# Background products of a Hymba block at every fourth step of the big matmuls, two pairs of heads side by side

## The chip, the cores and the metric

One core of one Trainium2 chip runs one launch of the kernel. The time is device microseconds for the launch. TensorE (PE in the profile) does matmuls, VectorE (DVE) and ScalarE (ACT) work on elements, GpSimd (POOL) and SyncE (SP) mostly issue transfers. Each engine works through its instructions in a fixed order; an instruction that waits holds up all that stand behind it on its engine.

## The reference

One layer of a decoder block on 512 tokens of width 2048, all in float32:

```python
h = rmsnorm(x) * (1 + scale1(c)) + shift1(c)
p = h @ w_in                                  # 2048 columns for the conv group, 3520 for RWKV
# A: val * sigmoid(gate), causal depthwise conv of 31 taps, group norm, silu       (16 heads of 64)
# B: token shift, then per head of 64:  S = S * w + (S a) b^T + v k^T ;  y = S r   (16 heads, 512 tokens)
#    group norm of y, + bonus (sum of r * k * r_k) * v, times the gate g
x = x + gate1(c) * (concat[A, B] @ w_out)
h = rmsnorm(x) * (1 + scale2(c)) + shift2(c)
x = x + gate2(c) * ((silu(h @ w1) * (h @ w3)) @ w2)      # d_ff = 5632
return rmsnorm(x)
# scale, shift and gate: six blocks of 2048 columns of c @ w_ada + b_ada
```

## The kernel before

**Big matmuls.** Every large product is done as three fp32r matmuls (high times high, high times low, low times high; `mm3`, line 74 does each). Weights arrive as 128x1024 blocks; `split` rounds a block on ACT (`wh`, line 92) and takes the rest on DVE (`wl`, line 93). A *step* is the work of one weight block on one accumulator, three matmuls with 512 columns. The program is a list of units of 16 steps: `in_units` (w_in, 37 units, 1776 big matmuls in the order `ORDER`), `out_units` (w_out, 16 units, 256 steps), `fast_units` (w1 and w3, a Strassen-like form) and `ff2_units` (w2).

**Background work.** All else of the mixer runs in the shadow of the steps. It is cut into generators that yield between pieces, and a `Lane` advances one generator: it waits as many steps as its table of waits says, then lets the next piece issue its instructions. Four lanes run at once. `scan` does `rwkv_scan` for a pair of heads, in halves of eight chunks of 64 tokens: products named `fp` and `yy` on TensorE, then `FV` (lines 780, 781) and the state `S` (line 792) on DVE. `pre` does `rwkv_pre` for the next pair: scaled keys, the masked products `gg`, `bk` and `npp`, transposes (line 639), and `inverse` of a triangular matrix. In the inverse, a 16x16 part is solved on DVE, goes through DRAM, is widened on POOL (`a`, line 719), and is then grown by a chain of products in the buffer `gg`. `cnv` does the 31 taps on DVE (line 843) and the norm of two heads of the conv group. `ada` makes rows or columns of the modulation, 512 columns per job: 16 multiply-adds of 128x512 on DVE (line 882), each on a block `wa` loaded from `w_ada`, and at the end a product with ones. The tables are `SCAN`, `PRE`, `CONV`, `ADA` and, in w_out, `ADA_ROWS`. Small products go to buffers `bk` (two), `gg` (one), `fp` and `yy`.

**Order.** `run()` sends the units through `stream`, and after every step it runs each lane once. A scheduler then places the instructions of each engine, and so the final order on an engine is not that of the code alone; it is shown below where it matters.

**Around w_out.** In unit 3 of w_out's first column block, `open_ff` finishes the first three lanes at once. Then four jobs remain: three rows of gate1 (column blocks 1 to 3), which `add_row` needs when a column block of w_out is done, and one job (`LATE = 1`) that makes the last quarter of `s2`, the columns of 1 + scale2. `open_h2`, ahead of the first ff1 unit, finishes what is left, folds `norm2_g` into `s2`, transposes x for tokens 0 to 255 (`make_a`, line 1108, scaled and shifted by `s2` and `sh2` into `raw`, line 1115) and makes the first ff1 operands. `scale` multiplies x by the row's rstd (line 1074). At the end of ff1, `last_hid` rounds the last hidden block into `hh` and `hl` for ff2, at a place named in the table `todo`.

Of the kernel before, what the change touches and what calls it, by code (L numbers as in the profile page):

```python
# [20 lines left out]
NT = T // P  # L21
CW = 1024
NB = CW // P
# [12 lines left out]
class Block:  # L36
# [912 lines left out]
    def run(self):  # L949
# [27 lines left out]
        pres = []  # L977
# [3 lines left out]
        for n, ps in zip("rkv", first):  # L981
# [4 lines left out]
        pres.append((0, dict(self.rkv)))  # L986
        self.gate = {}
        ada = lambda part, cc, out, fn: fn(part, cc, out)
        self.scan, self.pre, self.cnv = Lane(self.scans, self.rwkv_scan, SCAN), Lane(pres, self.rwkv_pre, PRE, PRE0), \
            Lane(self.convs, self.conv, CONV)  # L990
        lanes = self.lanes = [self.scan, self.pre, self.cnv, Lane(adas, ada, ADA)]


        def in_units():
# [28 lines left out]
        def open_ff():  # L1023
            own = lanes[:3]
            while any(l.busy for l in own):
                for l in own:
                    next(l)
            del lanes[:3]
            self.mix_back(KB)
            rps.close()  # L1030
            lops.close()
            self.xp = tops.enter_context(tc.tile_pool(name="xp", bufs=1))
            self.ff = ffs.enter_context(tc.tile_pool(name="ff", bufs=1))

            self.x1 = []
            load_x(0)
            self.rows = self.ff.tile([P, D], F32, name="rows", bufs=1)
            self.ss = self.ff.tile([P, NT, 8], F32, name="ss", bufs=1)[:, :, 0:4]
            rows = [(2, cc, lambda: self.rows, self.ada_rows) for cc in range(1, 4)]
            lanes[0].queue.extend(rows + late)  # L1040
            lanes[0].waits = lanes[0].first = ADA_ROWS
            self.fast_ws = fasts.enter_context(tc.tile_pool(name="wsp2", bufs=1, side="right"))

        def open_rows():
# [25 lines left out]
        def scale(c, t, engine):  # L1070
            o, rs = self.x1[c][:, t], self.rs[:, t:t + 1]
            if engine is nc.scalar:
                return engine.activation(out=o, in_=o, func=AF.Identity, scale=rs)
            return engine.tensor_scalar(out=o, in0=o, scalar1=rs, scalar2=None, op0=ALU.mult)
# [77 lines left out]
        def fast_units():  # L1152
            v, s = nc.vector, nc.scalar
            for c in range(NF // 4):
# [61 lines left out]
                for part in range(2):  # L1216
                    for u in range(4):
                        def stepped(j, part=part, u=u, c=c, turn=turn, end0=end0, end1=end1):
                            if c == 0 and part == 0 and u < 3 and j == 0:
                                for t in range(NT):  # L1220
                                    scale(u + 1, t, nc.scalar if u else nc.vector)
                            if c == 0 and part == 0 and u == 0 and j in (4, 5):
                                make_a(j - 4, (1,))
                            if c == 0 and part == 0 and u < 3 and j in (2, 7):
                                make_a(2 * u + 2 + j // 7)
                            if c == 0 and part == 0 and u == 3 and j in (7, 9):
                                make_b(j // 9)
                            if c == 0 and part == 1 and u < 3 and j in (1, 7):
                                make_b(2 * u + 2 + j // 7)
                            if c and part == 0 and u in (1, 2) and j in (1, 6):  # L1230
                                turn(2 * (u - 1) + j // 6)
                            if u == 3:
                                (end0, end1)[part](j)
# [20 lines left out]
        def get4(k):  # L1254
            f["four"] = k, self.ff.tile([P, 4, T], F32, name="hr", bufs=1)
            nc.gpsimd.dma_start(out=f["four"][1], in_=self.raw[k:k + 4].rearrange("k p t -> p k t"))
# [33 lines left out]

        def ff2_units():

            todo = {(0, 0, 0): [open_ff2], (0, 0, 4): [last_hid, load_x1, load_x1],
                    (0, 0, 8): [lambda: get4(12), load_x1, load_x1], (0, 1, 0): [lambda: split4(12), lambda: get4(16)],
                    (0, 1, 8): [lambda: split4(KB), lambda: get4(20)], (0, 3, 4): [lambda: split4(0), lambda: get4(24)],
                    (0, 3, 8): [lambda: split4(4), lambda: get4(28)], (1, 0, 0): [lambda: split4(8), lambda: get4(32)],
                    (1, 3, 8): [lambda: split4(12), lambda: get4(36)], (1, 3, 12): [lambda: split4(KB)]}
# [39 lines left out]
            yield from fast_units()  # L1337
            yield from ff2_units()

        for _ in self.stream(units()):  # L1340
            for l in lanes:
                l.run()

# [6 lines left out]

SCAN = (2, 2, 2, 3, 1, 1, 2, 3, 1, 1, 3, 2, 2, 2, 2, 2, 2, 1, 3, 2, 2)
PRE = (2, 2, 2, 2, 2, 2, 2, 2, 2, 2, 1, 2, 2, 2, 2, 3, 2, 8, 4, 2, 2, 2, 2, 1, 2, 2, 2, 1, 2)
CONV = (2, 2, 2, 2, 1, 2, 1, 2, 3, 3, 2, 2, 2, 2, 2, 2, 2, 3)
ADA = (4, 4, 4, 4, 4, 4, 4, 4, 4, 4, 4, 4, 4, 4, 4, 4, 4, 4, 6, 3, 3, 3)
ADA_ROWS = (2, 1, 2, 2, 2, 2, 2, 2, 3, 2, 3, 2, 2, 2, 2, 3, 2, 2, 4, 4, 2, 2)
PRE0 = PRE[:17] + (20,) + PRE[18:]  # L1360
LATE = 1

WS2 = 6
# [2 lines left out]
class Lane:  # L1366


    def __init__(self, queue, fn, waits, first=None):
        self.queue, self.fn, self.waits, self.first = queue, fn, waits, first or waits  # L1370
        self.job, self.n, self.wait, self.done = None, 0, 0, 0

    @property
    def busy(self):
        return bool(self.job or self.queue)

    def run(self):
        if self.wait:
            self.wait -= 1
        else:  # L1380
            next(self)

    def finish(self, n):

# [131 lines left out]
```

## Time and profile before

| what | value |
|---|---|
| median of 3 runs | 2484.78 us (2482.81 to 2487.75) |
| profiled execution | 2477.18 us, its span 2475.5 us |
| TensorE busy | 2373.9 us, 96% of the span |
| VectorE busy | 1784.8 us, 72% |
| ScalarE busy | 1048.3 us, 42% |
| head, up to the first w_in unit behind it | 0 to 158.6 us |
| w_in | 158.6 to 876.5 us |
| w_out | 876.5 to 1093.7 us |
| entry to ff1 | 1093.7 to 1104.0 us |
| ff1 | 1104.0 to 1983.2 us |
| ff2 | 1983.2 to 2475.5 us |

The span runs from the first instruction to the last one; the profiled execution lasts 1.7 us longer. The stages are read off TensorE's timeline by the names of its matmuls. A busy TensorE is not TensorE at its best: matmuls overlap one another, and their ends are modelled, so that the cost of a small product is read from the starts of the big matmuls on either side of it.

### The profile page before, as it was taken

Reading aid. Unit: us, or ns where it says so; the run is one execution under the profiler, and the core shown is the slowest. Engines: PE = TensorE matmul, PEld = TensorE weight load, DVE = VectorE, ACT = ScalarE, POOL = GpSimd, SP = SyncE. Lnnn points to the kernel's source line nnn. Section 1 sums busy time; section 2 is a strip of 40 time slices with the busy share of each in tenths; the row PEclk is TensorE's granted clock in tenths of the full one; section 3 lists DMA queues with packets and bytes.
Section 4 is the critical chain, followed back from the end, with each engine's and each line's share of the span. In section 5 each row is a group of like instructions: output and inputs, shape, how many; then the busy total and the mean of one; then the engine's idle time right before and its main releaser. Section 6 shows DMA issues by size and latency. Waiting matters only on the chain. (4 is left out here: it accounts for less than half of the span.)

```text
span 2475.5 us, 36145 instructions
## 1 busy us (share of the span) xinstructions
PE 2373.9 (96%) x13984; PEld 1864.0 (75%) x13984; DVE 1784.8 (72%) x2727; ACT 1048.3 (42%) x1521; POOL 137.3 (6%) x232
## 2 busy tenths in 40 slices
PE   5998999999999998989999999999999999999998
PEld 4766667767766676767888888888888878888886
DVE  4764888888888885679878777787777867534434
ACT  4253464464454443246544444444444432222223
POOL 2000100100100100000000000000000000000000
PEclk9999999999999998999999999999999999999999
DMA  9953245344354458756777777767777886423332
GB/s 335 346 174 94 74 124 144 92 134 127 88 147 114 124 175 281 246 193 197 254 254 216 235 238 239 232 206 232 239 234 241 297 285 228 145 97 118 98 102 102
DMA packets 339372, 464.30 MB, mean 188 GB/s; under 512 B 42979, under 2 KB 165073, under 8 KB 338176
## 3 DMA queue, kind: packets, MB, share of 16 engines
q1 hardware_dynamic: 331312, 436.64, 56.7%
q0 software_dynamic: 7888, 25.36, 2.7%
q8 instruction: 109, 1.79, 0.3%
q14 instruction: 63, 0.52, 0.1%
HBM read 431.52 MB, written 30.41 MB: 187 GB/s over the span
## 5 line engine op out<-in xcount | busy, mean ns | idle before, releaser
L92 ACT CAST wh<-ws 128x512 fp32r<-128x512 f32 (+1 forms) x696 | 547.7, 810 | 888.8 <-PE acc L74 310.8
L93 DVE TENSOR_TENSOR wl<-ws,wh 128x512 fp32r<-128x512 f32 (+1 forms) x696 | 642.2, 938 | 364.9 <-ACT wh L92 360.5
L74 PE MATMUL acc<-xh,wh 128*128 128x512 f32 x592 | 258.7, 437 | 2.8 <-ACT wh L92 2.8
L74 PE MATMUL acc<-xl,wh 128*128 128x512 f32 x592 | 241.9, 409 | 0.0
L74 PE MATMUL acc<-xh,wl 128*128 128x512 f32 x592 | 238.6, 403 | 0.0
L882 DVE SCALAR_TENSOR_TENSOR ada<-wa,sc,ada 128x512 f32<-128x512 f32 x256 | 192.4, 752 | 63.6 <-DMA wa<-in_w_ada_dram 53.2
L74 PE MATMUL b<-wh,xh 128*128 128x512 f32 x560 | 222.1, 397 | 0.7 <-ACT ada L895 0.7
L74 PE MATMUL acc<-wh,xh 128*128 128x512 f32 x552 | 221.7, 402 | 0.0
L74 PE MATMUL acc<-wh,xl 128*128 128x512 f32 x552 | 219.7, 398 | 0.0
L74 PE MATMUL b<-wl,xh 128*128 128x512 f32 x560 | 219.6, 392 | 0.0
L74 PE MATMUL b<-wh,xl 128*128 128x512 f32 x560 | 219.1, 391 | 0.0
L74 PE MATMUL acc<-wl,xh 128*128 128x512 f32 x552 | 218.4, 396 | 0.0
L1453 DVE TENSOR_TENSOR ws<-ws,ws 128x1024 f32<-128x1024 f32 x123 | 149.7, 1217 | 0.0
L74 PEld LDWEIGHTS acc<-xh,wh 128*128 128x128 f32 x592 | 111.9, 189 | 35.6 <-issue 5.3
L74 PE MATMUL b<-wh,x 128*128 128x512 f32 x352 | 136.9, 389 | 1.4 <-ACT wh L92 1.4
L74 PE MATMUL b<-wl,x 128*128 128x512 f32 x352 | 137.0, 389 | 0.0
L74 PE MATMUL b<-wh,raw 128*128 128x512 f32 x352 | 137.0, 389 | 0.0
L74 PEld LDWEIGHTS acc<-xh,wl 128*128 128x128 f32 x592 | 112.5, 190 | 27.2 <-issue 2.2
L74 PEld LDWEIGHTS acc<-xl,wh 128*128 128x128 f32 x592 | 112.6, 190 | 24.5 <-issue 5.8
L74 PEld LDWEIGHTS b<-wh,xh 128*128 128x128 f32 x560 | 105.6, 189 | 24.1 <-ACT ada L895 2.2
L74 PEld LDWEIGHTS acc<-wl,xh 128*128 128x128 f32 x552 | 105.2, 190 | 23.8 <-DVE wl L93 2.3
L74 PEld LDWEIGHTS b<-wh,xl 128*128 128x128 f32 x560 | 105.8, 189 | 22.6 <-issue 0.5
(415 smaller groups left out, 4221.1 us busy)
## 6 DMA issues: line engine op xcount, KB each, us to landing
ws<-in_w_ff_dram SPq DMA_DIRECT2D x440, 512.0 KB, 4.8
wa<-in_w_ada_dram SPq DMA_DIRECT2D x256, 256.0 KB, 3.7
ws<-in_w_in_dram SPq DMA_DIRECT2D x74, 512.0 KB, 3.9
wa<-in_w_ada_dram SPq DMA_DIRECT2D x32, 1024.0 KB, 11.9
ws<-in_w_out_dram SPq DMA_DIRECT2D x24, 512.0 KB, 5.2
rawd<-wa POOLq DMA_DIRECT2D x28, 256.0 KB, 4.9
hr<-rawd POOLq DMA_DIRECT2D x7, 1024.0 KB, 6.3
hidd<-wa POOLq DMA_DIRECT2D x24, 256.0 KB, 5.3
```

What stands on the lines that cost most here:

```text
L74: return self.nc.tensor.matmul(out, lhsT=lhsT, rhs=rhs, start=start, stop=stop, skip_group_check=True)
L92: self.nc.scalar.copy(out=hi, in_=x)
L93: return self.nc.vector.tensor_tensor(out=lo, in0=x, in1=hi.bitcast(F32), op=ALU.subtract).ins
L882: nc.vector.scalar_tensor_tensor(out=acc, in0=was[r], scalar=self.sc[:, r:r + 1], in1=acc, op0=ALU.mult, op1=ALU.add)
L1453: k.nc.vector.tensor_tensor(out=out, in0=a, in1=b, op=ALU.subtract)
```

## The change

Four things change.

1. **Slots.** A piece that issues small products now runs only at a *slot*, every fourth step (`SLOT = 4`; every second step while only one pair of heads is in work, at either end; no limit once the row buffers of w_out are open). Tables (`SCAN_BANKS`, `PRE_BANKS`, `CONV_BANKS`) say how many of the slot's two product buffers a piece takes. The lanes share them in turn, and a piece that finds too few left waits for a later slot. A wait of 0 runs the following piece in the same slot. The wait tables are new.
2. **Modulation in w_out.** The four jobs there advance by `ADA_OUT`, 58 steps per job, where `ADA_ROWS` took 50.
3. **Held-back scalings.** The four scalings of the second column block of x, in front of the first ff1 unit, are issued after the activation that `make_a(1, (0,))` ends with.
4. **`last_hid`** stands at point (0, 0, 8) of ff2, one unit of 16 steps behind (0, 0, 4), where it stood.

```diff
@@ run()
-        self.scan, self.pre, self.cnv = Lane(self.scans, self.rwkv_scan, SCAN), Lane(pres, self.rwkv_pre, PRE, PRE0), \
-            Lane(self.convs, self.conv, CONV)
-        lanes = self.lanes = [self.scan, self.pre, self.cnv, Lane(adas, ada, ADA)]
+        self.scan, self.pre, self.cnv = Lane(self.scans, self.rwkv_scan, SCAN, None, SCAN_BANKS), \
+            Lane(pres, self.rwkv_pre, PRE, PRE0, PRE_BANKS), Lane(self.convs, self.conv, CONV, None, CONV_BANKS)
+        lanes = self.lanes = [self.scan, self.pre, self.cnv, Lane(adas, ada, ADA, None, {20: 1})]
...
-            lanes[0].waits = lanes[0].first = ADA_ROWS
+            lanes[0].waits = lanes[0].first = ADA_OUT
...
-                                for t in range(NT):
-                                    scale(u + 1, t, nc.scalar if u else nc.vector)
+                                with self.tc.issue_after(self.last_fn) if not u else nullcontext():
+                                    for t in range(NT):
+                                        scale(u + 1, t, nc.scalar if u else nc.vector)
...
-            todo = {(0, 0, 0): [open_ff2], (0, 0, 4): [last_hid, load_x1, load_x1],
-                    (0, 0, 8): [lambda: get4(12), load_x1, load_x1], (0, 1, 0): [lambda: split4(12), lambda: get4(16)],
+            todo = {(0, 0, 0): [open_ff2], (0, 0, 4): [load_x1, load_x1],
+                    (0, 0, 8): [last_hid, lambda: get4(12), load_x1, load_x1], (0, 1, 0): [lambda: split4(12), lambda: get4(16)],
...
-        for _ in self.stream(units()):
+        for n, _ in enumerate(self.stream(units())):
+
+            ends = self.pre.done + bool(self.pre.job) in (1, NB)
+            if ends and self.pre.done:
+                self.cnv.waits = self.cnv.first = CONV_END
+            free = 2 if self.rowp is not None or n % (2 if ends else SLOT) == 0 else -1
             for l in lanes:
-                l.run()
+                free = l.run(free)
...
-SCAN = (2, 2, 2, 3, 1, 1, 2, 3, 1, 1, 3, 2, 2, 2, 2, 2, 2, 1, 3, 2, 2)
-PRE = (2, 2, 2, 2, 2, 2, 2, 2, 2, 2, 1, 2, 2, 2, 2, 3, 2, 8, 4, 2, 2, 2, 2, 1, 2, 2, 2, 1, 2)
-CONV = (2, 2, 2, 2, 1, 2, 1, 2, 3, 3, 2, 2, 2, 2, 2, 2, 2, 3)
+SLOT = 4
+SCAN = (1, 1, 1, 1, 1, 1, 1, 1, 1, 1, 1, 1, 1, 1, 1, 1, 2)
+PRE = (2, 2, 2, 2, 2, 2, 2, 0, 1, 1, 1, 6, 0, 2, 0, 2, 0, 8, 8, 2, 2, 2, 2, 2, 0, 1)
+CONV, CONV_END = (3,), (2,)
...
+ADA_OUT = (2, 1) + (3, 3, 2) * 5 + (3, 4, 4, 2, 2)
...
@@ class Lane
-    def run(self):
+    def run(self, free):
+
         if self.wait:
             self.wait -= 1
-        else:
+            return free
+        while True:
+            need = self.banks.get(self.n if self.job else 0)
+            if need is not None:
+                if need > free:
+                    return free
+                free -= need
             next(self)
+            if not self.job or self.wait >= 0:
+                self.wait = max(self.wait, 0)
+                return free
```

What the change makes of the order is seen on the engines. **TensorE in w_in**, while the third pair of heads is prepared and the second is scanned. `acc` are big matmuls, `bk<-ident,bk` the transposes, `fp` and `yy` the scan, `bk<-ar,bk` a group of products of the preparation. Before:

```order
L639 MATMUL bk<-ident,bk 128x64 x8
L74 MATMUL acc_2257<-xh_1256,wh 128x512
L74 MATMUL fp<-S,ar 64x64 x2
L74 MATMUL yy<-ar,S 64x64 x2
L74 MATMUL acc_2257<-xl_1257,wh 128x512
L74 MATMUL acc_2257<-xh_1256,wl 128x512
L74 MATMUL acc_2257<-xh_1261,wh 128x512
L74 MATMUL acc_2257<-xl_1262,wh 128x512
L74 MATMUL acc_2257<-xh_1261,wl 128x512
L74 MATMUL bk<-ar,bk 64x64 x13
L74 MATMUL yy<-Q,FV 64x64
L74 MATMUL bk<-ar,bk 64x64 x3
```

And the same pair after the change:

```order
L74 MATMUL acc_2421<-xh_415,wl 128x512
L74 MATMUL bk<-ar,bk 64x64 x16
L74 MATMUL fp<-S,ar 64x64 x2
L74 MATMUL yy<-ar,S 64x64 x2
L639 MATMUL bk<-ident,bk 128x64 x8
L74 MATMUL acc_2421<-xh_420,wh 128x512
L74 MATMUL acc_2421<-xl_421,wh 128x512
L74 MATMUL acc_2421<-xh_420,wl 128x512
L74 MATMUL acc_2421<-xh_517,wh 128x512
L74 MATMUL acc_2421<-xl_518,wh 128x512
L74 MATMUL acc_2421<-xh_517,wl 128x512
L74 MATMUL acc_2421<-xh_522,wh 128x512
```

The transposes, the scan and the group, which were three bursts with big matmuls in between, stand side by side as one, and twelve big matmuls separate it from the next burst. (The trace counts two passes for each small product of float32 that is counted here once, and one for each transpose.)

**VectorE in w_in**, at the same kind of place: where the preparation makes `r` (line 617), which the product of the bonus reads. `f` is the end of the scan of the pair before (lines 812, 813, 818), `kn<-gg` (line 597) masks the first product of the inverse. Before:

```order
L588 TENSOR_TENSOR bk<-kn,pi 128x8x64
L812 SCALAR_TENSOR_TENSOR f<-yy,colB,f 128x512
L597 TENSOR_TENSOR kn<-gg,gm 128x512
L813 SCALAR_TENSOR_TENSOR f<-f,colB,bv 128x512
L93 TENSOR_TENSOR wl<-ws,wh 128x512
L602 TENSOR_TENSOR k<-k,a 128x512
L818 TENSOR_TENSOR f<-f,bk 128x512
L613 TENSOR_TENSOR bk<-k,pi 128x8x64
L93 TENSOR_TENSOR wl<-ws,wh 128x512
L93 TENSOR_TENSOR f<-f,bv 128x512
L617 SCALAR_TENSOR_TENSOR r<-r,colB,k 128x512
L93 TENSOR_TENSOR wl<-ws,wh 128x512
```

After:

```order
L588 TENSOR_TENSOR bk<-kn,pi 128x8x64
L602 TENSOR_TENSOR k<-k,a 128x512
L792 SCALAR_TENSOR_TENSOR S<-fp,pc,Sp 128x64
L613 TENSOR_TENSOR bk<-k,pi 128x8x64
L617 SCALAR_TENSOR_TENSOR r<-r,colB,k 128x512
L597 TENSOR_TENSOR kn<-gg,gm 128x512
L93 TENSOR_TENSOR wl<-ws,wh 128x512 x2
L780 TENSOR_TENSOR FV<-fp,NV 64x64
L781 TENSOR_TENSOR FV<-fp,NV 64x64
```

`r` stood nine operations behind line 588, among them the end of the scan and the mask; now three stand between them, and the mask comes after `r`.

**VectorE at the entry to ff1.** `ada<-wa` (line 882) are multiply-adds of the late job, `wl` 128x1024 (line 93) the rounding of the first ff1 weights, `tm` and `x` (lines 913, 915) the sums of w_out's last column block, line 902 the copy of the late columns and line 1082 the last touch to `s2`. Before, all of the job's multiply-adds stand ahead of that rounding:

```order
L93 TENSOR_TENSOR wl<-ws,wh 128x512 x2
L882 SCALAR_TENSOR_TENSOR ada<-wa,sc,ada 128x512 x3
L93 TENSOR_TENSOR wl<-ws,wh 128x1024
L1453 TENSOR_TENSOR ws_10014<-ws_10014,ws_10016 128x1024
L913 TENSOR_TENSOR tm<-b_9846,rows 128x512
L915 TENSOR_TENSOR x_9844<-x_9844,tm 128x512
```

After, eleven of the sixteen stand behind it, the last of them here:

```order
L1074 TENSOR_SCALAR x_9212<-x_9212,rs 128x512
L335 SCALAR_TENSOR_TENSOR rs<-newton,rs 128x1
L882 SCALAR_TENSOR_TENSOR ada<-wa,sc,ada 128x512
L1074 TENSOR_SCALAR x_9000<-x_9000,rs 128x512
L882 SCALAR_TENSOR_TENSOR ada<-wa,sc,ada 128x512
L1074 TENSOR_SCALAR x_9212<-x_9212,rs 128x512
L902 COPY s_131<-gg 128x4
L93 TENSOR_TENSOR wl<-ws,wh 128x1024
L1082 SCALAR_TENSOR_TENSOR s_131<-s_131,colB 128x16
```

The eleven moved from the middle of w_out's last units to its end, in between the sums and scalings of the last column block, and `s2` now follows them all.

## Rows read from the trace of the kernel before

**Rows 1.** Stages (windows): start:end, length, busy us per engine, PE clock, DMA share, GB/s.
```profile
158.60:876.50 717.90, 689.14 (x6246) 496.17 (x6246) 591.76 (x1120) 349.62 (x533) 74.78 (x90) 0.99 0.43 122
...
1093.70:1104.00 10.30, 2.98 (x15) 1.84 (x13) 8.46 (x31) 9.16 (x19) 1.15 (x2) 0.66 0.50 158
```

**Rows 2.** TensorE's waits in w_in: total us, times, longest.
```profile
PE bk L74 <- DVE r L617: 11.6, 7, 2.3
PE gg L74 <- POOL a L719: 8.3, 3, 5.7
PE gg L74 <- DVE a L736: 6.5, 5, 2.4
```

**Rows 3.** TensorE's timeline, one group of 32 passes 64x64 alone: start, us, instruction.
```profile
458.59 0.39 PE L74 MATMUL acc<-xh,wl 128*128 128x512 f32 x1
458.90 1.15 PE L74 MATMUL bk<-ar,bk 64*64 64x64 f32 x32
...
460.32 0.39 PE L74 MATMUL acc<-xl,wh 128*128 128x512 f32 x1
```

**Rows 4.** TensorE's timeline, two such groups side by side.
```profile
677.08 0.39 PE L74 MATMUL acc<-xl,wh 128*128 128x512 f32 x1
677.39 0.34 PE L74 MATMUL bk<-bkT,a 64*64 64x64 f32 x4
...
679.79 0.39 PE L74 MATMUL acc<-xh,wh 128*128 128x512 f32 x1
```

**Rows 5.** TensorE's timeline, eight transposes 64x128 alone.
```profile
450.79 0.39 PE L74 MATMUL acc<-xh,wl 128*128 128x512 f32 x1
451.11 0.71 PE L639 MATMUL bk<-ident,bk 64*128 64x64 f32 x8
...
452.08 0.39 PE L74 MATMUL acc<-xl,wh 128*128 128x512 f32 x1
```

**Rows 6.** TensorE's timeline, eight transposes followed by a 64x64 group.
```profile
188.06 0.40 PE L74 MATMUL acc<-xh,wh 128*128 128x512 f32 x1
188.38 0.71 PE L639 MATMUL bk<-ident,bk 64*128 64x64 f32 x8
...
190.44 0.39 PE L74 MATMUL acc<-xh,wl 128*128 128x512 f32 x1
```

**Rows 7.** TensorE's timeline, half a scan step alone, then one behind a full product.
```profile
407.31 0.39 PE L74 MATMUL acc<-xl,wh 128*128 128x512 f32 x1
407.63 0.33 PE L74 MATMUL fp<-S,ar 64*64 64x64 f32 x4
...
408.35 0.39 PE L74 MATMUL acc<-xh,wh 128*128 128x512 f32 x1
...
409.51 0.39 PE L74 MATMUL acc<-xh,wl 128*128 128x512 f32 x1
409.74 1.02 PE L74 MATMUL bk<-cy,cen 128*128 128x512 f32 x2
410.68 0.34 PE L74 MATMUL fp<-FV,bkT 128*64 128x64 f32 x4
...
411.41 0.40 PE L74 MATMUL acc<-xl,wh 128*128 128x512 f32 x1
```

**Rows 8.** TensorE's timeline, a full f32 product alone.
```profile
244.41 0.39 PE L74 MATMUL acc<-xh,wl 128*128 128x512 f32 x1
244.63 1.02 PE L74 MATMUL bk<-e,bo 128*128 128x512 f32 x2
...
245.72 0.40 PE L74 MATMUL acc<-xl,wh 128*128 128x512 f32 x1
```

**Rows 9.** TensorE's waits in w_out and behind it.
```profile
PE b L74 <- DVE ada L882: 5.1, 1, 5.1
```

**Rows 10.** Page, costliest groups: busy us, mean ns, idle before.
```profile
L882 DVE SCALAR_TENSOR_TENSOR ada<-wa,sc,ada 128x512 f32<-128x512 f32 x256 | 192.4, 752 | 63.6 <-DMA wa<-in_w_ada_dram 53.2
```

**Rows 11.** TensorE's waits at the entry to ff2.
```profile
PE acc L1200 <- DVE hl L93: 4.0, 1, 4.0
```

More of the change, by code (lines that the diff above doesn't have):

```diff
@@ L1351 @@
 OUT_ORDER = [[8, 9, 10, 11], [12, 13, 14, 0], [1, 2, 3, 4], [5, 6, 15, 7]]
-SCAN = (2, 2, 2, 3, 1, 1, 2, 3, 1, 1, 3, 2, 2, 2, 2, 2, 2, 1, 3, 2, 2)
-PRE = (2, 2, 2, 2, 2, 2, 2, 2, 2, 2, 1, 2, 2, 2, 2, 3, 2, 8, 4, 2, 2, 2, 2, 1, 2, 2, 2, 1, 2)
-CONV = (2, 2, 2, 2, 1, 2, 1, 2, 3, 3, 2, 2, 2, 2, 2, 2, 2, 3)
+SLOT = 4
+SCAN = (1, 1, 1, 1, 1, 1, 1, 1, 1, 1, 1, 1, 1, 1, 1, 1, 2)
+PRE = (2, 2, 2, 2, 2, 2, 2, 0, 1, 1, 1, 6, 0, 2, 0, 2, 0, 8, 8, 2, 2, 2, 2, 2, 0, 1)
+CONV, CONV_END = (3,), (2,)
+SCAN_BANKS = dict.fromkeys(range(1, 16), 0) | {17: 1, 18: 1}
+PRE_BANKS = {1: 2, 2: 1, 7: 0, 8: 1, 11: 1, 12: 1, 13: 1, 14: 1, 15: 1, 16: 1, 17: 1} | dict.fromkeys(range(19, 24), 0) \
+    | {24: 1, 25: 1}
+CONV_BANKS = {16: 1, 17: 1}
 ADA = (4, 4, 4, 4, 4, 4, 4, 4, 4, 4, 4, 4, 4, 4, 4, 4, 4, 4, 6, 3, 3, 3)
@@ L1366, with __init__ @@
 class Lane:
-    def __init__(self, queue, fn, waits, first=None):
-        self.queue, self.fn, self.waits, self.first = queue, fn, waits, first or waits
+    def __init__(self, queue, fn, waits, first=None, banks={}):
+        self.queue, self.fn, self.waits, self.first, self.banks = queue, fn, waits, first or waits, banks
         self.job, self.n, self.wait, self.done = None, 0, 0, 0
```

## Prediction, made before the changed kernel was run

> **What bounds the kernel now.** I read the page first, then the trace cut into stages by the names of TensorE's matmuls, then TensorE's waits stage by stage, then its timeline around single small products. TensorE is busy 96% of the span, so the time is the sum of what TensorE issues and the few places where it waits. Windows by stage: w_in, where nearly all edits act, lasts 717.9 us, with the clock at 0.99 and VectorE busy for 591.8 us, 82% [rows 1]. TensorE's waits there are short and mostly three: 11.6 us for `r`, 8.3 us for POOL's `a`, 6.5 us for the sums of the inverse [rows 2]. That is 26 us in all; the remainder of what w_in could give is in what the small products cost.
>
> That cost is not in the busy column. Undisturbed, big matmuls start every 0.232 us (five starts from 408.35 to 409.51) [rows 7]. I take as the cost of a burst of small products the time from the start of the last big matmul ahead of it to the start of the second one behind it, less 2 x 0.232 = 0.46 us. A group of 32 passes of 64x64 alone then costs 460.32 - 458.59 - 0.46 = 1.27 us [rows 3]. Eight transposes alone cost 0.83 us [rows 5], half a scan step alone 0.58 us [rows 7], and a full product of 128x512 in f32 alone 0.85 us [rows 8].
>
> **Small products side by side.** The products themselves are the same before and after: 152 passes of the full kind, the same groups, transposes and scan halves, counted in TensorE's order. Only the bursts between big matmuls are fewer: 286 before, 204 after. What a merger saves depends on what meets.
> - Two 64x64 groups side by side cost 679.79 - 677.08 - 0.46 = 2.25 us where two alone cost 2.54: 0.29 us saved [rows 3, 4].
> - Transposes and a 64x64 group, which use the array in another shape, cost 190.44 - 188.06 - 0.46 = 1.92 us where alone they cost 2.10: 0.18 us saved [rows 3, 5, 6].
> - A full product and a scan half cost 411.41 - 409.51 - 0.46 = 1.44 us, alone 0.85 + 0.58 = 1.43: nothing saved [rows 7, 8].
>
> So it is a change of the array's shape that costs, not the interruption: a full product runs in the shape of the big matmuls and saves nothing as a neighbour. Counted in the order, runs of the 64x64 shape fall from 145 to 118 and those of 128x64 from 84 to 79, runs of transposes stay at 16. That is 32 mergers of like shape x 0.29 = 9.3 us. Places where two unlike small shapes meet directly rise from 11 to 39: 28 x 0.18 = 5.0 us. The other 22 of the 82 vanished bursts merge with full products, at nothing. Sum: **-14.3 us**. Its bounds are 0, as for a full product, and 82 x 0.29 = 24 us if all save like the best row; I stay with the sum, since each kind has its row.
>
> The Trainium skill states in TensorEngine Tiling (Array Packing), Tiling Modes, Key Properties, that changing the tiling mode drains TensorE, while another tile of the same mode does not. The rows above agree. The order after has 92 fewer changes of shape; were each worth half of 0.29 us, as between like groups, the rule's sum would be 13 us.
>
> **The wait for `r`.** Before, `r` stands on VectorE behind the mask of the first inverse product and the scan's closing operations; the product that reads it waits up to 2.3 us, seven times [rows 2]. After, `r` stands three operations behind line 588, the mask comes later, and on TensorE twelve big matmuls lie between the burst ahead and the product of `r`. The wait should go: **-10 us**, with bounds 0 and -11.6.
>
> **The inverse.** The wait for POOL's `a` is mostly one of 5.7 us, the first pair's; the other two pairs reach that product 23 and 95 big matmuls later than before in the order, so their share goes: 8.3 - 5.7 = **-2.6 us**. The opposite holds for the chain in `gg`: each product needs a sum on VectorE made from the one ahead. Before, 13 to 16 big matmuls (3 to 3.7 us) lie between, and after, often 2 to 7 (0.5 to 1.6 us). Before, this wait was 6.5 us in five places [rows 2]; about as many get tighter. A loss between 0 and 6.5 us; I take **+4**. The VectorE work ahead of a late sum stays the same, so no more than the queue of one or two operations is at stake each time.
>
> **w_out.** At the second row of gate1 TensorE waits 5.1 us for the last multiply-adds [rows 9]. In the order after, that row's product stands 46 big matmuls later and the next row's 72 later (10.7 and 16.7 us at 0.232), more than the wait. It goes: **-5.1 us**, between 0 and that. What is late next is the fourth job, the late columns of `s2`. 208 steps are left in w_out; 4 x 50 fit, 4 x 58 = 232 don't. So eleven of its multiply-adds move behind the first rounding of ff1 weights, and `open_h2` issues them together.
>
> **The entry to ff1.** From the end of w_out to the first ff1 matmul it is 10.3 us now, and VectorE is busy 8.46 us of that [rows 1]: there is no room. Eleven multiply-adds at 0.752 us add 8.3 us to VectorE ahead of `s2`, and 11.0 us if each also waits for its load as on average (63.6 us over 256) [rows 10]. Two roundings of 128x1024 at 1.22 us, now ahead of `s2`'s end, fall behind it: -2.4. Then the ones product, the copy, `s2` and `raw` follow in a chain. Net +5.9 to +8.6, to which overlap with the last units of w_out adds a gain and the chain behind the last multiply-add a loss; I take **+8**, with bounds +3 and +14. The held-back scalings lie in this gap on VectorE; they move past `raw`'s activation and are hidden under the gap: 0. Without that cover they would cost 4 x 0.48 us.
>
> **`last_hid`.** TensorE waits 4.0 us for `hl` [rows 11]. The product now comes one unit later (16 steps of 0.7 us), but on VectorE six multiply-adds of the last modulation row stand ahead of `hl`, where one did; they go at the pace of their loads. Between -4 and +3; I take **-1**.
>
> **Sum.** -14.3 - 10 - 2.6 + 4 - 5.1 + 8 - 1 = **-21 us**, against the profiled execution of 2477.2: 2456. The runs' median stands 7.6 us above that execution, so the forecast for the runs is 2484.8 - 21 = **2464 us**.
>
> **Rivals.**
> - *Every burst counts.* If the break in the stream of big matmuls itself costs, each vanished burst saves the fixed part, about 0.4 us (0.58 us for a scan half of eight short passes, less 8 x 0.02). Then 82 x 0.4 = 33 us instead of 14, in sum -40: **2445 us**. For it: scan halves, the commonest burst, are nearly all fixed part. Against it: the full product next to the scan saves nothing [rows 7, 8]. Chance 0.14.
> - *VectorE takes the gain back.* VectorE is busy 82% in w_in on average [rows 1], and the slots gather more of its work at one moment: two groups' masks, copies and scan sums come due together. Then waits for `FV`, `S` or the sums of the inverse take the place of those for `r`, about 0.15 us at each of some 100 slots: +15, in sum -6: **2479 us**. For it: little slack in the inverse stretches. Against it: twelve big matmuls (2.8 us) between slots cover a sum of 0.2 to 0.8 us. Chance 0.15.
> - *Slower.* The scan is a chain: product, `FV`, product, `S`. If its pieces no longer meet their operands, TensorE waits in each of 128 slots for a VectorE queue of one 128x512 operation, half of it on average, 0.37 us [rows 10]: +47, in sum +26: **2511 us**. It decides from 0.16 us per slot, where the -21 is gone. Against it: halves lie four steps apart after, and two or three before, with almost no wait for `S` then. Chance 0.04.
> - *The change does nothing*: the scheduler might have undone the slots. The order shows that it did not; what remains is that both shape costs and waits were mis-read and their sum is near 0, **2485 us**. Chance 0.05.
>
> **How the numbers follow.** Forecast 0.62, the rivals 0.14, 0.15, 0.04 and 0.05, in their order. The forecast's own range has the mergers at 8 to 20 us, the inverse at 0 to 6.5 and the entry at 3 to 14, not all at the same end: 2454 to 2473. The range for 8 in 10 takes in most of the first rival and the better half of the second: 2447 to 2478. About 0.2%, 5 us, can be told from no change: faster (below 2480) holds the forecast, the first rival and 0.10 of the second, 0.86; same, the rest of the second and most of the case of no effect, 0.09; slower 0.05.
>
> **What would show it.** In the changed kernel's profile: w_in about 24 us shorter; no wait for `r`; transposes directly beside 64x64 groups at about 1.9 us; a group beside another at 2.25 us; no wait of 5 us in w_out; a gap of about 18 us ahead of the first ff1 matmul, ended by `raw`; ff1 within 1 us as before. It would be wrong if the waits for `gg`, `FV` or `S` together are above 15 us in w_in, if merged bursts cost as much as they do apart, or if the entry to ff1 costs more than 14 us.

## The result, and the profile after

The changed kernel takes 2457.24 us (median of 4 runs, 2451.47 to 2459.04), the kernel before 2483.8 us in the same comparison. The ratio is 0.9898, 95% interval 0.988 to 0.9916: about 25 us faster. The forecast was 2464 with a range of 2447 to 2478. In the profiled executions the span falls from 2475.5 to 2449.4 us, by 26.0, where the sum had 21.

First the same stages as in [rows 1]: start and end of the stretch, its length, busy time of PE, PEld, DVE, ACT and POOL, TensorE's clock, share of DMA, GB/s. The rows are w_in, w_out, the entry to ff1, and ff2.

```profile
157.62:849.82 692.20, 664.11 (x6246) 491.80 (x6246) 575.31 (x1119) 350.82 (x533) 74.69 (x89) 0.99 0.44 126
849.82:1057.89 208.07, 198.79 (x892) 154.09 (x890) 143.65 (x237) 72.40 (x129) 10.51 (x21) 0.97 0.70 234
1057.89:1074.20 16.31, 5.76 (x25) 4.48 (x25) 12.86 (x39) 10.82 (x22) 0.93 (x2) 0.62 0.51 162
...
1951.55:2449.40 497.85, 478.66 (x2093) 392.83 (x2091) 239.90 (x396) 132.08 (x246) 6.08 (x9) 0.98 0.43 144
```

w_in is 692.2 us long in place of 717.9 and the entry 16.3 in place of 10.3 [rows 1]; w_out has lost 9 us and ff2 has gained almost 5. A table of all traces stands below. Then TensorE's waits in w_in, to be set beside [rows 2]:

```profile
PE fp L74 <- DVE S L792: 7.8, 8, 2.2
PE gg L74 <- POOL a L719: 7.3, 5, 2.0
...
PE gg L74 <- DVE a L736: 2.8, 2, 2.6
PE bk L74 <- DVE Q L650: 2.2, 1, 2.2
PE bk L74 <- DVE r L617: 2.0, 3, 0.9
```

The wait for `r` has gone from 11.6 us to 2.0, as forecast. But waits for `S`, 7.8 us in eight places, and for `Q` have come, so that the rows of this view add up to 31.0 us for w_in where they were 31.5: hardly less. TensorE's idle time says the same: 717.9 - 689.1 = 28.8 us before [rows 1], 692.2 - 664.1 = 28.1 after. What w_in gained lies in the bursts, and for a smaller part in the clock: in the records of the granted clock, 20.2 us of w_in run at half clock (1.2 in place of 2.4 GHz) before and 10.0 after. Of the bursts, one, a scan half, eight transposes and a 64x64 group in a row on TensorE, reads:

```profile
357.55 0.39 PE L74 MATMUL acc<-xh,wl 128*128 128x512 f32 x1
357.87 0.34 PE L74 MATMUL fp<-FV,bkT 128*64 128x64 f32 x4
...
358.25 0.71 PE L639 MATMUL bk<-ident,bk 64*128 64x64 f32 x8
358.89 1.15 PE L74 MATMUL bk<-ar,bk 64*64 64x64 f32 x32
...
360.30 0.39 PE L74 MATMUL acc<-xl,wh 128*128 128x512 f32 x1
```

By the prediction's measure it costs 360.30 - 357.55 - 0.46 = 2.29 us, where alone the three cost 0.58 + 0.83 + 1.27 = 2.68 [rows 3, 5, 7]: 0.39 us saved at two places where unlike shapes meet. And one of like shapes, a scan half that is woven into two 64x64 groups:

```profile
362.60 0.39 PE L74 MATMUL acc<-xh,wl 128*128 128x512 f32 x1
362.91 0.27 PE L74 MATMUL fp<-S,ar 64*64 64x64 f32 x2
...
364.08 0.98 PE L74 MATMUL bk<-FV,e 64*64 64x64 f32 x27
...
365.32 0.39 PE L74 MATMUL acc<-xl,wh 128*128 128x512 f32 x1
```

It costs 365.32 - 362.60 - 0.46 = 2.26 us, as much as the two groups without it [rows 4]; alone it would be 0.58 + 2 x 1.27 = 3.12. Here 0.86 us are saved, more than the 2 x 0.29 of the prediction: the eight passes of the scan half cost nothing at all. Why, no run shows.

### The profile page after: what moved, and what is told of

It reads as the page before. It is cut to its first block, busy times and chain, and to the rows that moved or that the text cites. A ratio compares the mean times of both kernels' runs of the same rounds, so it can differ in the third digit from the quotient of the medians.

```text
span 2449.4 us, 36135 instructions
## 1 busy us (share of the span) xinstructions
PE 2347.8 (96%) x13984; PEld 1859.8 (76%) x13984; DVE 1768.2 (72%) x2727; ACT 1049.0 (43%) x1521; POOL 138.2 (6%) x232
## 3 DMA queue, kind: packets, MB, share of 16 engines
q8 instruction: 109, 1.79, 0.3%
## 5 line engine op out<-in xcount | busy, mean ns | idle before, releaser
L74 PE MATMUL acc<-xl,wh 128*128 128x512 f32 x592 | 236.1, 399 | 0.0
L74 PEld LDWEIGHTS b<-wh,xh 128*128 128x128 f32 x560 | 105.6, 189 | 28.1 <-ACT ada L895 5.1
L74 PEld LDWEIGHTS b<-wl,xh 128*128 128x128 f32 x560 | 105.7, 189 | 21.9 <-issue 1.0
```

The costliest lines, as they stand in the source:

```text
L74: return self.nc.tensor.matmul(out, lhsT=lhsT, rhs=rhs, start=start, stop=stop, skip_group_check=True)
```

## Experiments

The lengths of the stages in the traces, in us, cut at the same matmuls (ff1 ends at its 3741st big matmul), with the time in w_in at half clock (from the records of the granted clock), the median of the timed runs and its ratio to the kernel before:

| kernel | w_in | at half clock | w_out | entry | ff1 | ff2 | median | ratio (95%) |
|---|---|---|---|---|---|---|---|---|
| before | 718.0 | 20.2 | 217.2 | 10.3 | 878.3 | 493.2 | | |
| changed | 692.2 | 10.0 | 208.1 | 16.3 | 877.4 | 497.9 | 2457.24 | 0.9898 (0.988 to 0.9916) |
| E1 slots only | 694.7 | 17.1 | 223.2 | 10.8 | 877.8 | 492.8 | 2456.48 | 0.9911 (0.989 to 0.9931) |
| E2 the rest only | 723.2 | 27.3 | 204.0 | 16.4 | 876.8 | 498.5 | 2482.04 | 1.0022 (1.0005 to 1.0039) |
| E3 scan offset | 706.1 | 33.7 | 208.3 | 17.0 | 878.1 | 499.9 | 2464.86 | 0.9947 (0.993 to 0.9965) |
| E4 r's product later | 733.0 | 64.0 | 215.0 | 8.4 | 877.6 | 492.0 | 2488.5 | 1.0039 (1.0021 to 1.0056) |
| E5 full dummies | 713.5 | 13.0 | 207.5 | 17.4 | 878.3 | 499.6 | one execution, 2475.24 | |
| E6 64x64 dummies | 728.7 | 9.7 | 210.3 | 16.9 | 878.1 | 499.1 | one execution, 2493.68 | |
| E7 last_hid back | 693.7 | 10.2 | 212.0 | 16.2 | 877.5 | 492.8 | 2454.03 | 0.9887 (0.9868 to 0.9906) |
| E8 old table in w_out | 698.1 | 23.2 | 220.3 | 10.7 | 877.9 | 497.4 | 2463.56 | 0.9924 (0.9901 to 0.9947) |
| E9 52 steps a job | 692.1 | 13.7 | 215.2 | 10.9 | 877.9 | 489.8 | 2451.66 | 0.9882 (0.986 to 0.9903) |
| E10 51 steps a job | 694.9 | 16.5 | 218.3 | 9.8 | 877.5 | 491.0 | 2451.35 | 0.9885 (0.9864 to 0.9906) |
| E11 changed, again | 695.2 | 16.4 | 208.1 | 16.6 | 877.0 | 496.7 | 2454.58 | 0.9896 (0.9876 to 0.9916) |
| E12 r written first | 736.9 | 47.8 | 218.3 | 8.3 | 878.1 | 491.1 | 2493.89 | 1.0057 (1.0035 to 1.0078) |

Seven traces have the same work in w_in (changed, E1, E7 to E11): 692.1 to 698.1, mean 694.4. Two of the old one (before, E2) have 718.0 and 723.2. So a single w_in is known to some 3 us either way, and the gap of 26 us is well outside that. Most of the scatter goes with the clock: the seven follow their time at half clock, from 692 to 694 us with 10 to 14 of it to 698.1 us with 23.2. At half clock big matmuls start 0.43 us apart in place of 0.23 (the rows stand at E7), so that, as an estimate, 1 us at half clock costs 1 - 0.23 / 0.43 = 0.46 us where TensorE sets the pace. Of the 26 us between the means, 720.6 and 694.4, the clock is then about 4: (23.8 - 15.3) x 0.46.

**E1 and E2: the two halves of the change.** E1 has the slots and their tables alone, E2 the other three edits alone. E1 is the changed kernel less these:

```diff
-            lanes[0].waits = lanes[0].first = ADA_OUT
+            lanes[0].waits = lanes[0].first = ADA_ROWS
...
-                                with self.tc.issue_after(self.last_fn) if not u else nullcontext():
...
-            todo = {..., (0, 0, 4): [load_x1, load_x1], (0, 0, 8): [last_hid, ...
+            todo = {..., (0, 0, 4): [last_hid, load_x1, load_x1], (0, 0, 8): [...
```

> The kernel before with the slots and their tables alone; the modulations of w_out, the scalings and last_hid stand as before. If the gain is the small products and waits of w_in, w_in is 692 us long as in the changed kernel (before 718), the entry to ff1 falls back to about 10 us, and the whole is 24 to 28 us under before. If the other three edits carry part of it, w_in is as short but the whole is less than 20 us under before.

> The kernel before with the other three edits alone (modulations spread in w_out, held-back scalings, last_hid later). By my reading: w_in 718 us as before, w_out 5 to 9 us shorter, the entry to ff1 6 us longer, ff1 and ff2 together 0 to 4 us longer, in sum within 4 us of before. The rival, that these edits give a gain of their own: 5 us or more under before.

E1 keeps the short w_in (694.7) and the short entry. It is 23.2 us under before by medians; 24 to 28 were expected. E2 has an unshortened w_in and a median 2.4 us above before (0.05% to 0.39% slower). Nearly the whole gain is the slots'. But the parts of E2 are not small, they cancel: w_out -13.2, entry +6.1, ff2 +5.3. And they work on what the slots make worse: with the slots alone w_out grows by 6 us. Windows of w_out, E1 and then E2:

```profile
852.22:1075.38 223.16, 205.70 (x901) 158.16 (x899) 148.58 (x243) 72.04 (x128) 10.38 (x20) 0.94 0.68 224
```

```profile
880.75:1084.76 204.01, 197.06 (x894) 152.78 (x891) 142.99 (x236) 72.11 (x128) 10.07 (x20) 0.98 0.72 238
```

TensorE is idle 223.2 - 205.7 = 17.5 us in E1's w_out and 7.0 in E2's, at a clock of 0.94 and of 0.98. Half clock goes with the waits: 27.3 us of E1's w_out run at it and 6.8 of E2's, where the kernel before has 20.5. Against before, E2 has 6.6 us less idle time and 13.7 us less at half clock, worth 6.3 at 0.46 each: together 12.9 of its 13.2.

**E3: the same, but not side by side.** The scan's pieces run two steps away from the slot of the others:

```diff
             free = 2 if self.rowp is not None or n % (2 if ends else SLOT) == 0 else -1
+            if self.rowp is None and not ends and lanes[0] is self.scan:
+                self.scan.run(2 if n % SLOT == 2 else -1)
+                for l in lanes[1:]:
+                    free = l.run(free)
+                continue
```

> The changed kernel, but the scan's pieces run two steps behind the slot of the others, so that they don't meet: TensorE's order in w_in and w_out has 255 bursts in place of 204 (286 before), with all tables and spacings the same. If a change of the array's shape costs, only the mergers of a scan half with 64x64 groups and transposes are lost, about 24 of the 51, and w_in is 9 to 12 us longer than the changed kernel's 692. If every break of the big matmuls costs about 0.4 us, all 51 count: 20 to 22 us longer. If the mergers were worth nothing and the waits everything, w_in stays at 692.

The window of its w_in:

```profile
159.22:865.33 706.11, 680.55 (x6246) 498.30 (x6247) 573.07 (x1119) 350.68 (x533) 74.08 (x89) 0.98 0.43 124
```

706.1 us is 13.9 longer than the changed kernel's trace and 11.7 longer than the mean of the seven, and the median is longer too, 2464.86 against 2457.24. The 20 to 22 us of the break are far. The 9 to 12 of the theory of the shape hold it by the mean, but that is in part luck: E3 has 33.7 us at half clock where the seven have 15.3 on average, which at 0.46 each is worth 8.4 of the 11.7. The length alone does not tell the 9 to 12 of the shape from the 0 of the waits. The bursts do. Taken over all bursts of w_in, with the prediction's measure and each product priced as it costs alone, being neighbours saves 3.4 us before, 17.9 in the changed kernel (17.6 to 18.1 in the other traces with that w_in) and 10.3 here; other ways of pricing mixed bursts move each by up to 4 us and leave their order. Of the 7.6 us that E3 loses in this way it gets some 2.5 back as shorter waits: TensorE idles 706.1 - 680.6 = 25.5 us against 28.1.

**E5 and E6: the price of a break, and of a shape.** The changed kernel with one small added product between every two slots of w_in, 132 in the traces (131 were expected), whose result nobody reads:

```diff
...
+            if n % 4 == 2 and n < 592 and (self.scan.job or self.scan.done):
+                self.mm(self.fp[:, 256:320], self.ident, self.cen[:, 0:64], True, True)                    # E5
+                self.mm(self.fp[0:64, 256:320], self.ident[0:64, 0:64], self.cen[0:64, 0:64], True, True)  # E6
```

> The changed kernel with 131 added products in w_in, one between every two slots (two passes of 64 columns, float32, result not used), that use the whole 128x128 array. If a change of the array's shape costs and the mere break does not, each costs about an eighth of a full product's 0.85 us, 0.1 us: w_in about 14 us longer than the changed kernel's 692, at most 25. If every break costs about 0.4 us: 55 us longer or more.

> The same 131 added products at the same places and of the same length, but each uses one 64x64 quarter of the array. By either theory one alone costs about 0.46 us, as a pair of such passes does in the kernel before: w_in 50 to 62 us longer than 692. What tells is the difference to the same products with the whole array: 35 us or more if the shape is what costs, under 10 if it is the break.

One such product on TensorE's timeline, E5 with the whole array, then E6 with a quarter of it:

```profile
336.10 0.39 PE L74 MATMUL acc<-xh,wl 128*128 128x512 f32 x1
336.33 0.33 PE L74 MATMUL fp<-cen,ident 128*128 128x64 f32 x2
336.46 0.48 PE L74 MATMUL acc<-xh,wh 128*128 128x512 f32 x1
336.78 0.39 PE L74 MATMUL acc<-xl,wh 128*128 128x512 f32 x1
```

```profile
334.90 0.39 PE L74 MATMUL acc<-xh,wl 128*128 128x512 f32 x1
335.22 0.33 PE L74 MATMUL fp<-cen,ident 64*64 64x64 f32 x2
335.48 0.50 PE L74 MATMUL acc<-xh,wh 128*128 128x512 f32 x1
335.81 0.39 PE L74 MATMUL acc<-xl,wh 128*128 128x512 f32 x1
```

E5's costs 336.78 - 336.10 - 0.46 = 0.22 us, E6's 335.81 - 334.90 - 0.46 = 0.45. The median over those that stand alone, some 85 in each trace, is 0.22 and 0.45 too. Between the same passes in the one shape and in the other lie 0.23 us, for two changes of shape: 0.12 us each. The break with its two passes is 0.22: twice the 0.1 that was expected of it, and not 0.4. So the theory of the break fails. But the size on the whole was wrong: E6 was expected 50 to 62 us longer and is 34 longer than the mean, E5 19, so that the two differ by 15, between the 35 of the one theory and the 10 of the other. The single products decide between them, not the sums. (The clock does not blur this pair: 13.0 and 9.7 us at half clock.) The windows say where the time went:

```profile
157.31:870.76 713.45, 696.66 (x6510) 528.58 (x6511) 571.08 (x1121) 351.23 (x533) 73.03 (x89) 0.99 0.43 122
```

```profile
158.76:887.48 728.72, 716.45 (x6510) 510.19 (x6511) 571.88 (x1121) 351.50 (x533) 72.56 (x89) 0.99 0.42 120
```

TensorE's idle time is 713.5 - 696.7 = 16.8 us in E5 and 12.3 in E6, against 28.1 in the changed kernel. What is added on TensorE is in part paid from its waits; that VectorE catches up meanwhile is the likely reason. By the rows, 132 x 0.22 - 11.3 = 17.7 us for E5, near the 19; 132 x 0.45 - 15.8 = 43.6 for E6, more than the 34, since some of the 132 stand beside other small products.

**E4 and E12: the wait for `r` by itself.** Two ways of taking it out of the kernel before, with no merger. E4 lets TensorE come later, by one table; E12 lets VectorE make `r` earlier, ahead of the mask:

```diff
-PRE = (2, 2, 2, 2, 2, 2, 2, 2, 2, 2, 1, 2, 2, 2, 2, 3, ...        # E4
+PRE = (2, 2, 2, 2, 2, 2, 2, 2, 2, 2, 7, 1, 1, 1, 1, 2, ...
```

```diff
+        s.activation(out=a, in_=a, func=AF.Identity, scale=one("k_a"), bias=c["ok_a"][:, b:b + 1])    # E12
+        v.tensor_tensor(out=k, in0=k, in1=a, op=ALU.mult)
+        v.tensor_tensor(out=bk[:, :, 1], in0=ch(k), in1=ch(pi), op=ALU.mult)
+        v.tensor_tensor(out=ar[:, :, 1], in0=ch(r), in1=pe_[:, :, 1:C + 1], op=ALU.mult)
+        v.scalar_tensor_tensor(out=r, in0=r, scalar=one("r_k"), in1=k, op0=ALU.mult, op1=ALU.mult)
         M = rp.tile([P, NC, C], F32, name="kn")
         v.tensor_tensor(out=M, in0=mp, in1=mask(0), op=ALU.mult)
         inv = self.inverse(M)
```

(E12 drops the five lines from where they stood, behind the mask, so that the lines behind them have a number lower by one.)

> The kernel before with one table changed: the product that reads r is issued six steps later behind r, so TensorE reaches it 9 to 17 big matmuls later (2 to 4 us), and no products are merged. If the wait for r (11.6 us) is time lost, it is gone and w_in is 8 to 11 us shorter than before's 718. If TensorE would lose that time at the next product anyway, since VectorE as a whole is late there, w_in is within 3 us of before and the wait appears at the products behind it.

> The kernel before with k, its scaled copies and r written ahead of the mask of the first inverse product in the preparation, as the changed kernel has them on VectorE; TensorE's order stays as before but for the product of r, which comes 5 big matmuls sooner, and nothing is merged. If r is late because the mask stands ahead of it and sets off two 128x512 operations on POOL during which VectorE's take 1.7 us in place of 0.7, the wait for r falls from 11.6 to under 4 us and w_in is 6 to 10 us shorter than before's (718 and 723 us in two traces). If VectorE's lateness as a whole is what TensorE waits for, the wait moves to the inverse (its mask is later now) or to the products behind r, and w_in stays within 3 us.

TensorE's waits in E4's w_in, the first rows:

```profile
PE gg L74 <- POOL a L719: 11.0, 3, 6.3
PE bk L639 <- DVE bv L622: 8.4, 5, 2.3
PE bk L74 <- DVE bv L622: 3.2, 1, 3.2
```

And in E12's:

```profile
PE gg L74 <- POOL a L718: 30.3, 6, 6.0
PE gg L74 <- DVE a L735: 3.4, 2, 2.9
...
PE bk L74 <- DVE r L600: 2.1, 2, 1.2
```

In both the wait for `r` is gone, and in both the time is not: w_in is 733.0 and 736.9 us, longer by 10 and 14 us than the longer of the two old traces. In E4 11.6 us (8.4 + 3.2) are waited one product on, for `bv`, which VectorE makes from the product of `r`; in the kernel before that was 0.9. In E12 the mask is later, and with it the inverse that it starts: the wait for POOL's `a` goes from 8.3 us [rows 2] to 30.3. My first theory, that this wait is time lost that can be taken out, fell with E4; my second, that it was the mask's place alone, with E12. What E12's w_in is longer by is covered by idle time, 736.9 - 697.5 = 39.4 us against 28.8, and by the clock, 47.8 us at half against 20.2. E4's waits add up to about those of before; what is lower is its clock, 0.96 in the window of its w_in against 0.99 [rows 1]. The windows of w_in, E4 and E12:

```profile
157.03:890.06 733.03, 703.63 (x6238) 509.03 (x6239) 581.48 (x1120) 349.05 (x532) 78.62 (x90) 0.96 0.42 119
```

```profile
158.45:895.39 736.94, 697.46 (x6246) 504.56 (x6246) 585.30 (x1120) 349.77 (x533) 78.56 (x90) 0.97 0.42 119
```

Where E4's clock is lower, its trace shows. Behind five of its six waits for `bv`, 1.5 to 3.2 us long, it falls to half for 6.8 to 13.7 us, 44 us in all. Of the four waits of 2.3 us for `r` in the kernel before, one is followed by 3.4 us at half clock and three by none. One of each, the wait on TensorE's timeline and the window behind it, E4 and then before:

```profile
653.33 0.70 PE L639 MATMUL bk<-ident,bk 64*128 64x64 f32 x8 [2.19 <-DVE bv L622]
654.70:668.20 13.50, 13.37 (x104) 9.78 (x104) 8.50 (x15) 4.92 (x7) 3.38 (x4) 0.50 0.28 59
```

```profile
636.63 1.13 PE L74 MATMUL bk<-r,bo 128*128 128x512 f32 x2 [2.29 <-DVE r L617]
636.60:650.10 13.50, 13.47 (x140) 9.95 (x142) 11.33 (x37) 3.18 (x6) 0.00 (x0) 1.00 0.39 114
```

At 0.46 each the 44 us are worth 20, more than all that E4's w_in is longer by. Why the clock falls behind one wait and not behind another of the same length, no run here tells apart.

**E7: `last_hid` back at its place.**

```diff
-                    (0, 0, 8): [last_hid, lambda: get4(12), load_x1, load_x1], ...
+            todo = {..., (0, 0, 4): [last_hid, load_x1, load_x1], (0, 0, 8): [lambda: get4(12), ...
```

> The changed kernel with last_hid where it was. By the trace the later place saves 3.7 us at the last transposes of ff1, and 8 us are lost 40 us later in ff2, where TensorE waits 4.9 us for a row of gate2. If that loss comes of the move (the time in which the loads of that row were running is gone), then undoing it brings the 4 us wait for hl back and removes the wait for the row: in sum 2 to 5 us less than the changed kernel. If the loss comes from elsewhere, it stays, and the whole is 3 to 5 us more.

TensorE's waits from the end of ff1 on in the changed kernel, and then in E7:

```profile
PE acc L74 <- DVE ada L882: 4.9, 1, 4.9
PE acc L1200 <- DVE hl L93: 1.8, 1, 1.8
```

```profile
PE acc L74 <- DVE ada L882: 2.9, 2, 2.1
PE acc L1200 <- DVE hl L93: 2.7, 1, 2.7
```

ff2 is 492.8 us in E7 and 497.9 in the changed kernel. It doesn't depend on one trace: the seven with the early place (before, E1, E4, E7, E9, E10, E12) have 489.8 to 493.2, the seven with the late one (changed, E2, E3, E5, E6, E8, E11) 496.7 to 499.9. So the later `last_hid` costs 5 us, though the wait for `hl` is shorter as meant. The changed kernel waits 4.9 us for a row of gate2 in place of 2.9, and behind that wait the clock is down. Window from the wait on:

```profile
2009.50:2022.00 12.50, 7.59 (x20) 5.00 (x19) 7.63 (x13) 0.88 (x2) 0.52 (x1) 0.73 0.61 206
```

Its clock is 0.73: 6.8 us of it are at half, where E7 has none until its last 10 us, and there big matmuls start 0.43 us apart in place of 0.23:

```profile
2017.60 0.63 PE L74 MATMUL acc<-wh,xl 128*128 128x512 f32 x1
2018.03 0.63 PE L74 MATMUL gg<-wh,xh 128*128 128x512 f32 x1
...
2021.51 0.40 PE L74 MATMUL b<-wh,xh 128*128 128x512 f32 x1
2021.75 0.39 PE L74 MATMUL b<-wl,xh 128*128 128x512 f32 x1
```

By medians E7 (2454.03) is 3 us under the changed kernel, which these runs do not tell from none. That the loads of that row come late since less time is left for them was argued and not tried by itself.

**E8 to E11: the fourth modulation job.** E8 is the changed kernel with `ADA_ROWS` in w_out (50 steps a job); E9 and E10 have `last_hid` back and tables of 52 and 51 steps; E11 is the changed kernel beside them.

```diff
-ADA_OUT = (2, 1) + (3, 3, 2) * 5 + (3, 4, 4, 2, 2)
+ADA_OUT = (2, 1) + (2, 3, 2) * 5 + (3, 4, 4, 1, 2)        # E9
+ADA_OUT = (2, 1) + (2, 2, 2) * 5 + (2, 7, 6, 1, 2)        # E10
```

> The changed kernel with the old table for the modulations in w_out (50 steps a job, so that the fourth is done inside w_out). If the drained fourth job is what lengthens the entry to ff1, the entry falls from 16.3 to about 10 us and the waits for rows in w_out return (5 to 9 us): in sum within 3 us of the changed kernel. If the spread is needed to keep w_out from waiting, the whole is 5 us or more above the changed kernel.

> The changed kernel with last_hid where it was, and the four modulation jobs of w_out spread over 52 steps each in place of 58, so that four fit into the 208 steps left; two multiply-adds of the last job in place of eleven stand behind the first ff1 rounding. If the drained job lengthens the entry, it falls from 16.3 to about 11 us; if rows then come late in w_out, 3 to 5 us of it are waited there. With ff2 back at 493 us (from 498) the whole is 5 to 10 us under the changed kernel; if the entry doesn't shrink or w_out takes all of it, 4 to 5 us from last_hid alone.

> The same with 51 steps a job, the multiply-adds two steps apart and the product with ones 13 steps behind the last of them, where the other has about 8 steps and wider spacing. If the rows in w_out are late because their loads run at the memory's pace and the product comes too soon behind them, this has no wait over 2 us for rows in w_out and an entry of about 11 us: 8 to 12 us under the changed kernel. If issuing the loads sooner makes them slower or steals from the weights of w_out, the waits of 3 to 5 us stay and it equals the one with 52 steps.

> The changed kernel once more, on the chip of the other two, for comparison: w_in 690 to 698 us, the entry 16 to 17, ff2 497 to 500, 0.9 to 1.2% under before.

The entry follows the job in all of them: 16 to 17 us where eleven of its multiply-adds are drained, 10 to 11 where the job ends inside w_out. But w_out and the entry together are 224.4 to 228.2 us in the six traces with the slots and 58 steps (changed, E3, E5, E6, E7, E11), 226.1 with 52, 228.1 with 51, and 231.0 and 234.0 with 50 (E8, E1). Against 50 steps, the 6 us at the entry are less than what w_out pays in waits and half clock when the rows are hurried, and E8 is 6 us above the changed kernel by its median, and their runs do not overlap: some spread is needed. (From E7 to E1, which lacks the spread and the held-back scalings, it is only 2.4 us by medians.) Between 58, 52 and 51 steps these traces tell nothing. In E10, which was to remove the wait, TensorE waits 5.0 us for a row in w_out: so a product that comes too soon, here 13 steps behind the last multiply-add, was not the cause; what is, stays open. E9 and E10 have the lowest medians, 2451.66 and 2451.35, against E11's 2454.58 on the same chip; their runs overlap, and 3 us are within what is not told apart. The 5 to 12 us that were expected of them did not come: what they gain is ff2, from `last_hid`, and w_out takes back what the entry gives.

## Why the prediction was right, step by step

- **The small products (-14.3): right, in sum and mechanism.** Neighbours save 17.9 us in w_in in place of 3.4: -14.5. E3's bursts lose half of it with the mergers alone, and E5 and E6 show that it is the shape of the array, 0.12 us a change, and not the break. At that price the prediction's 92 changes are 11 us; the rest is in the split, which was off: full products indeed saved nothing as neighbours, unlike shapes were as sized, but a scan half woven into 64x64 groups saves up to 0.86 us where 2 x 0.29 was taken. The Trainium skill's rule from TensorEngine Tiling (Array Packing), Tiling Modes, Key Properties, that a change of tiling mode drains TensorE, agrees with E5 and E6: 0.22 us without a change and 0.45 with two.
- **The waits of w_in (-10 - 2.6 + 4 = -8.6): the sum was near by luck, its terms were not.** `r` lost 9.6 us of wait and POOL's `a` 1.0, but not as reasoned: the first pair's wait of 5.7 us, which was to stay, became 2.0, and the others, which were to go, rose from 2.6 to 5.3. The sums of the inverse lost 3.7 where I had +4; `S` and `FV` gained 8.4, `Q` 1.9, which I had put into a rival only. The view's rows add up to 31.5 and 31.0. E4 and E12 show that the step was wrong as reasoned: the wait for `r` is where VectorE's and the inverse's lateness shows, and taken out by itself it comes back one product on. Taken over all bursts, delays beyond the price alone fell from 43.2 to 34.7 us, by 8.5, but hardly any of that is waits. The clock is the largest part, a term that the sum lacked: 10.2 us less at half clock, 4.7 us at 0.46 each, and as the seven traces have 10.0 to 23.2 us of it, part of this is chance. About 3 us more, with the pieces priced alone, are products that a big matmul cuts in two, of which there are fewer. TensorE's idle time fell by 0.7.
- **w_out (-5.1): the wait's name was right, its price too small.** w_out fell by 9.1 us in the changed kernel and by 13.2 in E2. I took the wait of 5.1 us [rows 9] and left out the half clock that goes with the waits: it falls from 20.5 us to 13.7 and, in E2, to 6.8. I also put what the slots do to w_out at nothing; in E1 they lengthen it by 6.0.
- **The entry (+8): right**, +6.1, within its bounds. A gap of 18 us was forecast, and it is 16.3.
- **`last_hid` (-1): wrong**, by its sign and beyond its bounds: +4.7 in ff2. The step that failed is that I followed the wait for `hl` and not the modulation row behind it, which is late next; the wait of 4.9 us with its half clock is there. E7 shows it.
- **The scalings (0)** were not tried by themselves; E1 and E2 bound them only together with the others.
- Sum in the traces: head -1.0, w_in -25.8 (forecast -22.9), w_out -9.1 (-5.1), entry +6.1 (+8), ff1 and ff2 +3.8 (-1).

Of the rivals, *every burst counts* fell with E3, E5 and E6. *VectorE takes the gain back* was right in its mechanism, at 10.3 us of new waits for `S`, `FV` and `Q` rather than 15, but the old waits for `r`, `a` and the sums fell by 14.3. *Slower* and *the change does nothing* did not come. The first condition set for the forecast to be wrong, more than 15 us of waits for `gg`, `FV` and `S` in w_in, was met: 11.3 + 1.5 + 7.8 = 20.6 us. It was badly set, since the kernel before already had 15.9, and it missed that the bursts pay for more than that.

## What to carry to other kernels

Price a small product in a stream of big ones by the starts of the big ones on either side, not by its busy time, and put products that use the array in one shape next to each other; a product of the big matmuls' own shape can stand anywhere. A wait on an in-order engine is worth its length only if the chain behind it is early: follow it to the next product before counting it. And count the clock behind each wait with it: before two lengths of a stage are compared, compare their time at half clock, or a difference of the clock is taken for one of the kernel.

## What the runs showed of the hardware

Not expected: while POOL works on 128x512 operands, most of VectorE's operations of that size take more than twice as long. In the kernel before, of 14 that lay almost wholly beside such POOL operations in w_in, 11 took 1.39 to 1.79 us and three 0.67 to 0.75. A further case, which lies beside two POOL operations in turn, stands behind the mask that starts the inverse; POOL's timeline and then VectorE's:

```profile
630.77 1.74 POOL L698 TENSOR_TENSOR e<-kn,m 128x512 f32<-128x512 f32 x1
```

```profile
631.28 1.78 DVE L602 TENSOR_TENSOR k<-k,a 128x512 f32<-128x512 f32 x1
632.98 0.67 DVE L818 TENSOR_TENSOR f<-f,bk 128x512 f32<-128x512 f32 x1
```

`k` took 1.78 us, 1.2 of them beside POOL's operation of 1.74, and the next one, of the same size, 0.67. In the kernel before `r` stands behind `k` on VectorE and is that much later. In the changed kernel, where `k` stands ahead of the mask, its longest is 0.69 us; there it is `r` that runs into POOL now and then (up to 1.80 us).
